# Attention units alternated with value and output projection blocks, probabilities scaled on GpSimd, and a reordered start

## The chip, the cores and the metric

One core of a Trainium2 chip runs the whole program. The metric is device time in microseconds (us) of one launch. TensorE (PE) multiplies matrices, VectorE (DVE) and ScalarE (ACT) do the elementwise work, GpSimd (POOL) small helpers, and the SP queue issues nearly all loads.

## The reference

Two layers of a backbone act on 384 tokens (128 of context, 256 latent) of width 1024. A layer is: modulated norm, SwiGLU feed-forward (1024 to 2816 and back), modulated norm, token mixer, modulated norm, a second feed-forward. Shift, scale and gate come from a conditioning vector, one for context and one for latent tokens (adaLN).

```python
h = rmsnorm(x) * (1 + sc2) + sh2
u = h @ w_in                                   # Hyena 768, neighbourhood q k v 3 x 384, grouped q 384, k v 2 x 128
y_hy = x0 * (irfft(rfft(z) * rfft(filter)) + z * skip)       # z = x1 * v after a 3-tap convolution
y_na = softmax(q @ k.T / 8 + bias, local window + cached context) @ v     # 6 heads of 64
y_gq = softmax(rope(q) @ rope(k).T / 8, window + context + sink) @ v      # 6 query heads, 2 key heads
x = x + g2 * (concat(y_hy, y_na, y_gq) @ w_out)
```

The filter comes from a small network with two sine layers and does not depend on x. Outputs are x and the new keys and values of the context tokens.

## The kernel before

Everything lies transposed: xT holds 8 chunks of 128 features by 384 tokens. Each weight block is loaded in fp32 into one of NRAW raw buffers, split into a rounded part hi and a remainder lo (`split`, L134 to L136: ACT copies, DVE subtracts), and every product is three matmuls: hi by hi, hi by lo, lo by hi (`mm3`, L294 to L298). The blocks stand in one list, `jobs` (L138 on). `get` (L178) takes the next one; `ahead` (L165) splits up to three blocks further and issues the loads up to NRAW ahead on the SP queue, which also carries the adaLN weights and the attention biases.

adaLN work is 256 "halves": a 128x1024 DVE product with sum (L199) of a loaded weight block and the activated conditioning. `ada_tick(rate)` (L242) runs them at written rates (RATE, MIXRATE, SLOTADA); `need` (L248) runs a missing one on the spot when an update or a norm wants it.

`start` (L1157) prepares the first feed-forward block: the filter network (`Filters`, L517: two sine layers, taps, spectra), the sum of squares of xT (`square_chunk`, L314, and `stats1`, L328), and the first modulations by matmul (`chunk_load`, `chunk_rows`, `chunk_cols`). Engines take their instructions in program order, so the order in `start` is the order of each queue.

`mixer` (L616) runs the six groups of the input projection. Its background work consists of generators in a list `bg`; `work(budget)` (L619) advances each by one step, front first, while the budget lasts, and `drain` runs one to its end. Generators: `hyena` (convolution, then `fft`), `na_post` (norm of q and k), `gk_post` and `gq_post` (norm and rotation of the grouped heads). After the value projection vN (L1093) q, k and Hyena are drained (L1095 to L1097). Then 15 calls of `slot` (L999) run twelve attention units as a pipeline: in slot s unit s is scored (`un_score`), unit s-1 scaled by the reciprocal of its sum (`un_norm`, L892 to L900, on DVE), the pair ending in unit s-3 multiplied with the values (`un_pv`), unit s-2 transposed (`un_turn`), unit s exponentiated (`un_exp`). A unit holds two heads and either two query blocks (context and the first latent block) or one:

```python
hs = [unit(kind, i, qi) for kind in "NG" for i in range(3) for qi in range(2)]      # L996
for c, (pr, w) in enumerate(u.pr[e]):                                              # L899
    V.tensor_scalar(pr[:, :w], pr[:, :w], rec[:, e * n + c:e * n + c + 1], None, op0=ALU.mult)
```

The grouped generators are drained after six slots. Between slots stand three blocks of the output projection (`wout_block`, L1099), after them the rest. The layer-0 filter spectrum kft[0] sits in the buffer that later holds the transposed probabilities (L587).

## Time and profile before

| what | value |
|---|---|
| median of 3 runs (lowest, highest) | 1557.25 us (1556.47, 1557.54) |
| the profiled execution, its span | 1557.04 us, 1555.3 us |
| PE busy, DVE, ACT, POOL | 1503.2, 1131.0, 671.9, 73.1 us |
| mean granted PE clock | 0.988 |
| HBM read | 257.34 MB, 167 GB/s |

The span runs from the first to the last instruction. A granted clock of 1.00 is 2.4 GHz, the other level is 1.2 GHz. Large matmuls overlap in pairs, so their rate is read from counts over a stretch. Boundaries of stretches: the first feed-forward matmul starts at 45.99 us, the layer-0 mixer at 332.85, its first unit at 433.71, the second feed-forward block at 519.58; the layer-1 mixer at 1084.69, its first unit at 1185.08, the last feed-forward block at 1270.11.

### The profile page before, as it was taken

Reading aid. Unit: us, or ns where it says so; the run is one execution under the profiler, and the core shown is the slowest. Engines: PE = TensorE matmul, PEld = TensorE weight load, DVE = VectorE, ACT = ScalarE, POOL = GpSimd, SP = SyncE. Lnnn points to the kernel's source line nnn. Section 1 sums busy time; section 2 is a strip of 40 time slices with the busy share of each in tenths; the row PEclk is TensorE's granted clock in tenths of the full one; section 3 lists DMA queues with packets and bytes.
Section 4 is the critical chain, followed back from the end, with each engine's and each line's share of the span. In section 5 each row is a group of like instructions: output and inputs, shape, how many; then the busy total and the mean of one; then the engine's idle time right before and its main releaser. Section 6 shows DMA issues by size and latency. Waiting matters only on the chain.

```text
span 1555.3 us, 22995 instructions
## 1 busy us (share of the span) xinstructions
PE 1503.2 (97%) x8616; PEld 1443.7 (93%) x8616; DVE 1131.0 (73%) x2123; ACT 671.9 (43%) x1229; POOL 73.1 (5%) x194
## 2 busy tenths in 40 slices
PE   5999999999979999999999999999998899999998
PEld 2799999999957999999999999999996699999998
DVE  5468888868877788877757898787788667544444
ACT  4533333336556454333435333334465655333221
POOL 0000000011400000000000000000141000000000
PEclk9999999999989999999999999999999999999999
DMA  8555665655422435555543566566453024443442
GB/s 288 183 209 211 223 229 205 215 196 182 116 72 75 153 140 199 210 208 205 193 159 122 190 241 233 180 231 214 157 155 100 25 97 145 139 139 109 152 153 71
DMA packets 89288, 261.46 MB, mean 168 GB/s; under 512 B 10134, under 2 KB 27096, under 8 KB 89048
## 3 DMA queue, kind: packets, MB, share of 16 engines
q1 hardware_dynamic: 88792, 258.95, 48.5%
q8 instruction: 67, 1.10, 0.3%
q0 software_dynamic: 384, 1.05, 0.2%
q14 instruction: 45, 0.37, 0.1%
HBM read 257.34 MB, written 2.62 MB: 167 GB/s over the span
## 4 chain that ended last, share of the span: by engine, by line
PE 82%; DVE 10%; ACT 5%; issue 2%; DMA 1%; SPq 0%; POOL 0%; DVEq 0%; ACTq 0%; POOLq 0%
PE up L298 14%; PE up L296 14%; PE up L297 14%; PE dn L296 8%; PE dn L297 8%; PE dn L298 8%; PE pj L296 3%; PE pj L298 2%; PE pj L297 2%; DVE wlo L136 2%; ACT whi L135 1%; DVE junk L199 1%; DVE ml L136 1%; DVE pr L900 1%; DVE pr L923 1%
## 5 line engine op out<-in xcount | busy, mean ns | idle before, releaser
L136 DVE TENSOR_TENSOR wlo<-raw,whi 128x1024 fp32r<-128x1024 f32 (+2 forms) x352 | 394.4, 1125 | 131.1 <-ACT whi L135 130.7
L296 PE MATMUL up<-mh,whi 128*128 128x384 f32 (+1 forms) x1408 | 479.3, 340 | 2.6 <-ACT mh L135 2.6
L298 PE MATMUL up<-mh,wlo 128*128 128x384 f32 (+1 forms) x1408 | 477.7, 339 | 0.7 <-DVE wlo L136 0.5
L297 PE MATMUL up<-ml,whi 128*128 128x384 f32 (+1 forms) x1408 | 477.6, 339 | 0.4 <-DVE ml L136 0.4
L135 ACT ACTIVATE whi<-raw 128x1024 fp32r<-128x1024 f32 (+2 forms) x352 | 338.7, 975 | 263.6 <-PE dn L297 125.8
L199 DVE CUSTOM_DVE_ANT_0 junk<-adaw,cb,sml 128x1024 bf16<-128x1024 f32 x256 | 332.4, 1298 | 1.9
L296 PEld LDWEIGHTS up<-mh,whi 128*128 128x128 f32 x1408 | 266.1, 189 | 4.8 <-ACT mh L135 3.3
L298 PEld LDWEIGHTS up<-mh,wlo 128*128 128x128 f32 x1408 | 266.2, 189 | 2.0 <-DVE wlo L136 2.0
L297 PEld LDWEIGHTS up<-ml,whi 128*128 128x128 f32 x1408 | 266.0, 189 | 1.6 <-DVE ml L136 1.2
L296 PE MATMUL dn<-gh,whi 128*128 128x384 f32 x704 | 237.4, 337 | 0.0
L297 PE MATMUL dn<-gl,whi 128*128 128x384 f32 x704 | 237.4, 337 | 0.0
L298 PE MATMUL dn<-gh,wlo 128*128 128x384 f32 x704 | 237.0, 337 | 0.0
L135 ACT ACTIVATE gh<-t 128x384 fp32r<-128x384 f32 x76 | 39.9, 525 | 271.8 <-DVE t L476 262.1
L297 PEld LDWEIGHTS dn<-gl,whi 128*128 128x128 f32 x704 | 132.3, 188 | 0.0
L298 PEld LDWEIGHTS dn<-gh,wlo 128*128 128x128 f32 x704 | 132.2, 188 | 0.0
L296 PEld LDWEIGHTS dn<-gh,whi 128*128 128x128 f32 x704 | 132.1, 188 | 0.0
L296 PE MATMUL pj<-whi,mh 128*128 128x384 f32 (+1 forms) x240 | 79.6, 332 | 1.1 <-DVE hyt L353 1.1
L476 DVE TENSOR_TENSOR t<-up,t 128x384 f32<-128x384 f32 x72 | 39.9, 554 | 55.2 <-PE up L298 55.0
L298 PE MATMUL pj<-whi,ml 128*128 128x384 f32 (+1 forms) x240 | 78.3, 326 | 0.0
L297 PE MATMUL pj<-wlo,mh 128*128 128x384 f32 (+1 forms) x240 | 78.1, 326 | 0.0
L136 DVE TENSOR_TENSOR gl<-t,gh 128x384 fp32r<-128x384 f32 x76 | 42.4, 558 | 45.0 <-ACT gh L135 45.0
L306 POOL TENSOR_SCALAR rs_r<-rs_r 128x3 int32<-128x3 int32 (+2 forms) x14 | 8.5, 607 | 1194.0 <-DVE rs_r L305 738.9
(220 smaller groups left out, 1585.4 us busy)
## 6 DMA issues: line engine op xcount, KB each, us to landing
raw<-w SPq DMA_DIRECT2D x184, 512.0 KB, 4.4
adaw<-ada SPq DMA_DIRECT2D x128, 512.0 KB, 3.5
raw<-w SPq DMA_DIRECT2D x64, 448.0 KB, 4.4
raw<-win SPq DMA_DIRECT2D x48, 384.0 KB, 4.0
raw<-w13a SPq DMA_DIRECT2D x32, 384.0 KB, 4.0
adw<-ada SPq DMA_DIRECT2D x32, 192.0 KB, 4.6
raw<-woa SPq DMA_DIRECT2D x16, 384.0 KB, 3.2
nab<-nab SPq DMA_DIRECT2D x24, 192.0 KB, 3.1
```

The lines of the kernel that those rows point to most:

```text
L135: S.activation(hi, src, AF.Copy)
L136: V.tensor_tensor(lo, src, hi.bitcast(F32), op=ALU.subtract)
L199: V.tensor_tensor_reduce(out=junk, in0=w, in1=cb[:, v, :], scale=scale, scalar=small("ada_b", (l * NADA + p) * KD + j), op0=ALU.mult, op1= ...
L296: T.matmul(out, ah, bh, start=start, stop=False)
L297: T.matmul(out, ah, bl, start=False, stop=False)
L298: T.matmul(out, al, bh, start=False, stop=stop)
L306: G.tensor_scalar(r.bitcast(I32), r.bitcast(I32), -1.0, float(0x5F3759DF), op0=ALU.mult, op1=ALU.add)
L476: V.tensor_tensor(t1, PQ[1][:, :NT], t1, op=ALU.mult)
L900: V.tensor_scalar(pr[:, :w], pr[:, :w], rec[:, e * n + c:e * n + c + 1], None, op0=ALU.mult)
L923: V.tensor_tensor_reduce(out=u.pr[e][0][0], in0=u.sc[e][:, :NT], in1=u.mask[e], scale=-1.0, scalar=3.0e38, op0=ALU.add, op1=ALU.min, accum ...
```

## The change

Ten of the fifteen slots get a piece of large matmuls behind them: the value projection is cut into four steps behind slots 0 to 3, and the first two groups of the output projection into pieces of 9 matmuls (one k block of one group). Hyena is not drained before the units but goes on as background, and ends before the pieces that read it. The scaling of probabilities moves from DVE to GpSimd. Rates of adaLN halves and the budgets of the background change; halves leave the slots. There are three raw buffers instead of four, and kft[0] has a tile of its own. In `start` the sine layers are cut in two so that squares stand between, the taps precede the sum of squares, the fix of tap row 0 goes from DVE to ACT, and three of eight spectrum parts are run inside the first three steps of the feed-forward block.

```diff
-NRAW = 4
+NRAW = 3
...
-RATE = ((0.76, 0.635), (0.63, 0.515), (0.69, 0.66), (0.065, 0))
-MIXRATE = ((0.75, 0, 0, 0), (0.45, 0, 0, 0))
-BUD = (1.55, 3.3, 1.3)
-SLOTADA = (6, 0.3, 0.0)
+RATE = ((0.8, 0.72), (0.63, 0.515), (0.69, 0.66), (0.065, 0))
+MIXRATE = ((0.75, 0, 0.5), (0.3, 0, 0.3))
+BUD = (2.0, 3.0, 1.9)
...
-    kft = [None, cst.tile([P, 6, HY], F32, name="kft1")]
+    kft = [cst.tile([P, 6, HY], F32, name=f"kft{l}") for l in range(DEPTH)]
...
-                for g in range(2):
-                    jobs += [(A["woa"][l, g, :, k * 768:(k + 1) * 768], 768) for k in (1, 2, 3, 0)]
+                for g, k in ((0, 1), (0, 2), (0, 3), (1, 1), (1, 2), (1, 3), (0, 0), (1, 0)):
+                    jobs.append((A["woa"][l, g, :, k * 768:(k + 1) * 768], 768))
...
-            dftl = rawp.tile([P, 1024], F32, tag="raw", name="dftl")
-            load(A["dft1"][:, 0:4], dftl.rearrange("p (i c) -> p i c", i=4))
-            self.dftl = dftl
             self.dft0 = load(A["dft0"][:, 0:2 * P], tt("dft0", w=2 * P))
+            self.dftl = [load(A["dft1"][:, i], tt("dftl", w=HY)) for i in range(4)]
...
         def first(self):
+            S.activation(junk[:, 0:1], ones[:, 0:1], AF.Sin)
             p1 = ps("f1")
             T.matmul(p1[:, :NT], self.fw1, self.feats, start=True, stop=True)
-            self.h1 = tt("h1", w=NT)
-            sin_layer(p1[:, :NT], 0, self.h1)
+            self.fb = sm("fbm", 2)
+            V.tensor_tensor(self.fb, small("fb", 0, 2), small("freq", 0, 2), op=ALU.mult)
+            self.arg = sin_arg(p1[:, :NT], 0, self.fb[:, 0:1])
 
         def second(self):
+            h1 = tt("h1", w=NT)
+            S.activation(h1, self.arg, AF.Sin)
             p2 = ps("f2")
             for l in range(DEPTH):
                 r = slice(l * HD, (l + 1) * HD)
-                T.matmul(p2[r, :NT], self.fw2[r], self.h1[r], start=True, stop=True)
-            self.h2 = tt("h2", w=NT)
+                T.matmul(p2[r, :NT], self.fw2[r], h1[r], start=True, stop=True)
             self.p2 = p2
-
-        def second_sin(self):
-            sin_layer(self.p2[:, :NT], 1, self.h2)
             self.wsd = [tt("wsd", w=HY) for _ in range(2)]
             V.tensor_tensor(self.wsd[0], self.w3[0], self.w3[1], op=ALU.add)
             V.tensor_tensor(self.wsd[1], self.w3[1], self.w3[0], op=ALU.subtract)
 
+        def third(self):
+            self.arg = sin_arg(self.p2[:, :NT], 1, self.fb[:, 1:2])
+
+        def fourth(self):
+            self.h2 = tt("h2", w=NT)
+            S.activation(self.h2, self.arg, AF.Sin)
+            self.sd = []
...
-            dec = self.decay[t].rearrange("p (o c) -> p o c", o=1)
             for l in range(DEPTH):
-                V.tensor_tensor(
-                    S2[:, :, l], pt[l].rearrange("p (i c) -> p i c", i=2), dec.to_broadcast([P, 2, HY]), op=ALU.mult
-                )
+                for i in range(2):
...
+                    for i in range(2):
+                        S.activation(S2[0:1, i, l], p0[l][0:1, :HY], AF.Copy, scale=-1.0 if i else 1.0)
...
+        def spectrum(self, ft, part):
+            which, row = ((0, False), (1, False), (0, True))[part]
...
+            for l in range(DEPTH):
+                d = kft[l][:, 3 * q + ft]
+                S.activation(d[0:1] if row else d, o[:, l * HY:(l + 1) * HY], AF.Copy, scale=sc[0:1] if row else sc)
...
+        class Project:
+            def __init__(self, n, kper):
+                self.n, self.kper, self.kb = n, kper, 0
+                self.pt = [ps(f"pj{t}", "a") for t in range(3)]
+
+            def step(self):
...
                 ahead()
-                ada_tick(MIXRATE[l][2])
+                self.kb += 1
...
+        def project(n, kper, budget):
+            pr = Project(n, kper)
+            for kb in range(KD // kper):
...
+                    work(budget)
...
+            res = pr.out()
+            work(budget)
+            return res
...
-        spare = ["a"]
+        spare = ["b"]
...
-                    V.tensor_scalar(pr[:, :w], pr[:, :w], rec[:, e * n + c:e * n + c + 1], None, op0=ALU.mult)
+                    nc.gpsimd.tensor_scalar(pr[:, :w], pr[:, :w], rec[:, e * n + c:e * n + c + 1], None, op0=ALU.mult)
...
-                pp = ps(f"pp{e}", spare[0] if TAGS[2] else "b")
+                pp = ps(f"pp{e}")
...
-            if s >= SLOTADA[0]:
-                ada_tick(SLOTADA[1 + l])
...
-        pkv = project(256, 4, lambda kb: work(BUD[1]))
+        pkv = project(256, 4, BUD[1])
         gk_it = add(gk_post(pkv), True)
-        pg = project(384, 2, whole)
-        gq_it = add(gq_post(pg))
-        vN = project(384, 2, whole)
-        nc.gpsimd.dma_start(out=A["o_nv"][l], in_=vN[0])
+        pg = project(384, 2, BUD[0])
+        gq_it = add(gq_post(pg), True)
+
+        held = {}
+
+        def piece(po, g, k):
+            kb, kk = divmod(k, 2)
+            if (g, kb) not in held:
+                held[g, kb] = get()
+            hi, lo = held[g, kb]
+            for i in range(3):
+                s = slice(kk * 384 + i * P, kk * 384 + (i + 1) * P)
+                mm3(po[i][:, :NT], (hi[:, s], lo[:, s]), Y[k], k == 2, k == 1)
+            if kk:
+                del held[g, kb]
+            ahead(state["cur"] + min(AHEAD, NSPL - len(held)))
+
         drain(q_it)
         drain(k_it)
-        drain(hy_it)
...
-        while slot_n[0] < 6:
+        pv = Project(384, 2)
+        for s in range(4):
             slot()
+            pv.step()
+        X["vN"] = pv.out()
+        nc.gpsimd.dma_start(out=A["o_nv"][l], in_=X["vN"][0])
+        po = [[ps(f"po{i}", "a") for i in range(3)]]
+        slot()
+        piece(po[0], 0, 2)
+        slot()
         drain(gk_it)
         drain(gq_it)
-        for _ in range(2):
+        for k in (3, 4, 5):
             slot()
-        spare[0] = "b"
-        po = [ps(f"po{i}", "a") for i in range(3)]
-        wout_block(po, 3, 0, 2)
-        while slot_n[0] < len(hs):
+            piece(po[0], 0, k)
             slot()
-        wout_block(po, 3, 1, 2)
-        while slot_n[0] < len(hs) + 3:
-            slot()
-        wout_block(po, 3, 2, 2)
-        wout_block(po, 3, 3, 2, False)
-        for i in range(3):
-            update(l, 5, i, po[i])
-            after(i)
+        slot()
+        piece(po[0], 0, 6)
+        slot()
+        spare[0] = "a"
+        po.append([ps(f"po{i}", "b") for i in range(3)])
+        piece(po[1], 1, 2)
+        slot()
+        for g, k in ((1, 3), (0, 7), (1, 4), (1, 5), (1, 6), (1, 7)):
+            piece(po[g], g, k)
+            work(BUD[2])
+            ada_tick(MIXRATE[l][2])
+        drain(hy_it)
+        for g in range(2):
+            for k in range(2):
+                piece(po[g], g, k)
+            for i in range(3):
+                update(l, 5, 3 * g + i, po[g][i])
+                after(3 * g + i)
+        po = [ps(f"po{i}", "ab"[i]) for i in range(2)]
+        for kb in range(2):
+            hi, lo = get()
+            for kk, i in order2(4, 2, kb == 1):
+                k = kb * 4 + kk
+                s = slice((kk * 2 + i) * P, (kk * 2 + i + 1) * P)
+                mm3(po[i][:, :NT], (hi[:, s], lo[:, s]), Y[k], k == 0, k == KD - 1)
+            if kb == 0:
+                ahead()
+                ada_tick(MIXRATE[l][2])
+        for i in range(2):
+            update(l, 5, 6 + i, po[i])
+            after(6 + i)
             if i == 0:
                 ahead()
...
     def start(j, mid=False):
+        F = filters
         if mid:
             if j in (1, 4):
                 chunk_rows((j + 2) // 3)
             return
         if j == 0:
-            F = filters
             F.load_a()
-            for c in range(KD // 2):
+            F.load_b()
+            for c in range(KD):
                 load(A["xT"][:, c], xT[c])
-            F.load_b()
-            for c in range(KD // 2, KD):
-                load(A["xT"][:, c], xT[c])
+            load(A["ct"], ct)
+            load(A["ident"], ident)
             F.load_c()
-            load(A["ident"], ident)
-            load(A["ct"], ct)
             chunk_load(0)
             issue(2)
             F.first()
-            for c in range(3):
+            for c in range(4):
                 square_chunk(c)
             F.second()
-            F.second_sin()
-            for c in range(3, KD):
+            square_chunk(4)
+            F.third()
+            for c in range(5, KD):
                 square_chunk(c)
+            F.fourth()
             S.activation(ct[:, :, 0:2], ct[:, :, 0:2], AF.Silu)
+            F.taps(0)
             r = stats1()
-            for t in range(3):
-                F.taps(t)
+            F.taps(1)
+            F.taps(2)
+            chunk_load(1)
             ada_tables(0)
-            chunk_load(1)
-            F.spectrum(0)
+            F.spectrum(0, 0)
+            F.spectrum(0, 1)
+            F.spectrum(0, 2)
             R = stats2(r)
-            start_x(0, R)
             ahead(1)
-            F.spectrum(1)
-            start_x(1, R)
             chunk_rows(0)
-            F.spectrum(2)
+            for c in range(3):
+                start_x(c, R)
+            F.spectrum(1, 0)
             chunk_cols(0)
+            F.spectrum(1, 1)
             start_h(0)
             start_h(1)
             ahead(2)
-            issue(3)
+            issue(4)
             chunk_load(2)
-            for c in range(2, KD):
+            for c in range(3, KD):
                 start_x(c, R)
             return
         if j in (2, 5):
             chunk_cols((j + 1) // 3)
         if j + 1 < KD:
             start_h(j + 1)
+        if j < 4:
+            F.spectrum(*((1, 2), (2, 0), (2, 1))[j - 1])
```

## Rows read from the trace of the kernel before

**Rows 1.** The page, part 1: busy us (share of the span), instructions.

```profile
PE 1503.2 (97%) x8616; PEld 1443.7 (93%) x8616; DVE 1131.0 (73%) x2123; ACT 671.9 (43%) x1229; POOL 73.1 (5%) x194
```

**Rows 2.** Busy us by stretch: PE, PEld, DVE, ACT, POOL; PEclk, DMA, GB/s.

```profile
73.00:332.85 259.85, 259.85 (x1485) 259.85 (x1483) 211.95 (x324) 99.18 (x150) 0.00 (x0) 1.00 0.61 218
332.85:433.71 100.86, 98.74 (x584) 95.58 (x583) 81.13 (x194) 51.67 (x105) 30.10 (x69) 1.00 0.51 156
433.71:492.07 58.36, 47.69 (x298) 32.10 (x297) 47.72 (x162) 38.43 (x115) 0.00 (x0) 0.88 0.12 42
519.58:541.18 21.60, 18.99 (x99) 18.23 (x99) 16.75 (x34) 8.55 (x18) 3.80 (x13) 0.92 0.58 199
1185.08:1242.77 57.69, 47.35 (x298) 32.17 (x298) 42.87 (x153) 38.08 (x115) 0.00 (x0) 0.88 0.13 42
1270.11:1287.69 17.58, 17.13 (x100) 16.71 (x99) 10.62 (x23) 8.41 (x18) 3.67 (x13) 1.00 0.46 156
```

**Rows 3.** PE in order of time, two units without waits: start, us, instruction.

```profile
464.58 0.92 PE L912 MATMUL sc<-kTG,qTG 64*128 64x384 f32 x4
465.43 0.87 PE L961 MATMUL pp<-ident,pr 128*128 128x128 f32 x6
466.06 0.42 PE L296 MATMUL po<-yh,whi 128*128 128x384 f32 x1
...
476.37 0.92 PE L912 MATMUL sc<-kTG,qTG 64*128 64x384 f32 x4
...
479.92 0.27 PE L963 MATMUL pp<-ident,pr 128*128 128x128 f32 x1
```

**Rows 4.** What PE waited for, whole span: us in total, times, longest.

```profile
PE gt L772 <- DVE ra L1034: 9.0, 2, 4.5
...
PE pp L961 <- DVE pr L900: 4.5, 6, 1.7
```

**Rows 5.** DVE busy with line 900 alone, layer 0's units.

```profile
433.71:492.07 58.36, 11.34 (x36) 0.88 0.12 42
```

**Rows 6.** DVE and POOL in order of time, layer 0's mixer.

```profile
340.31 1.28 DVE L199 CUSTOM_DVE_ANT_0 junk<-adaw,cb,sml 128x1024 bf16<-128x1024 f32 x1
...
340.49 1.15 POOL L306 TENSOR_SCALAR rs_r<-rs_r 128x3 int32<-128x3 int32 x1 [315.56 <-DVE rs_r L305]
...
346.55 0.20 POOL L310 TENSOR_SCALAR rs_t<-rs_t 128x3 f32<-128x3 f32 x1
...
379.71 0.23 POOL L310 TENSOR_SCALAR rs_t<-rs_t 128x18 f32<-128x18 f32 x1
```

**Rows 7.** Costliest DVE group, 519.58 to 541.18 us: busy us, mean ns.

```profile
L199 DVE CUSTOM_DVE_ANT_0 junk<-adaw,cb,sml 128x1024 bf16<-128x1024 f32 x5 | 6.5, 1290 | 0.1
```

**Rows 8.** Groups of the first feed-forward block, 73 to 332.85 us.

```profile
L199 DVE CUSTOM_DVE_ANT_0 junk<-adaw,cb,sml 128x1024 bf16<-128x1024 f32 x80 | 104.1, 1301 | 0.7
L136 DVE TENSOR_TENSOR wlo<-raw,whi 128x1024 fp32r<-128x1024 f32 (+2 forms) x65 | 76.5, 1176 | 12.7 <-ACT whi L135 12.7
L135 ACT ACTIVATE whi<-raw 128x1024 fp32r<-128x1024 f32 (+2 forms) x65 | 65.8, 1017 | 53.8 <-PE dn L297 24.5 <-issue 20.5 <-PE up L297 7.6
```

**Rows 9.** DMA issues, page part 6: KB each, median us to landing.

```profile
raw<-w SPq DMA_DIRECT2D x184, 512.0 KB, 4.4
```

**Rows 10.** The start in order of time, all engines.

```profile
9.95 10.16 SPq L103 DMA_DIRECT2D adw<-ada  x16
...
15.27 0.52 ACT L515 ACTIVATE h<-arg 128x384 f32<-128x384 f32 x1 [2.99 <-DVE arg L514]
...
19.50 1.44 PE L332 MATMUL pss<-ones,accq 128*128 128x1 f32 x6 [8.54 <-DVE accq L319]
...
28.03 2.93 PE L603 MATMUL kf<-taps,dft 128*128 128x512 f32 x6
...
39.55 3.70 PE L603 MATMUL kf<-taps,dftl 128*128 128x512 f32 x8
...
45.99 0.69 PE L296 MATMUL up<-mh,whi 128*128 128x384 f32 x1 [2.17 <-ACT mh L135]
```

114 lines of the change are left out of this document (35 added, 79 removed).

## The prediction

> **What bounds it now.** I read first the share of each engine, then the busy time by stretch, then, inside the stretches where TensorE (PE) is not full, the instructions in order of time and what they waited for. PE is busy for 97% of the span [rows 1], so the kernel is bound by PE and a change that neither adds nor drops large matmuls can only win or lose the time in which PE waits or runs at the low clock. Where the weights stream, nothing is left: the first feed-forward block issues 1485 matmul records in 259.85 us, 0.175 us each, at full clock, with PE busy throughout [rows 2]. The holes are elsewhere. The attention stretches of the two layers last 58.36 and 57.69 us with PE busy for 47.7 and 47.4 at a granted clock of 0.88, a mix of the 2.4 and 1.2 GHz levels [rows 2].
>
> How much of such a stretch is excess: a key/query pair (a unit with two query blocks and one with a single one) costs PE 1.48 us for scores and transposes of the small unit and 480.19 - 476.37 = 3.82 us for scores, values and transposes of the large one when nothing is waited for, 5.3 us [rows 3]. Six pairs are 31.8 us; the 54 output-projection matmuls placed in the stretch are 54 x 0.175 = 9.45; nine transposes of the rotated queries some 0.9. That is 42.2 of 58.36 us: 16.2 us of excess in layer 0, 15.5 in layer 1. A visible piece of it is the wait for the rotated queries, 4.5 us in each layer, and smaller ones for the scaled probabilities [rows 4].
>
> **The change, part by part.**
>
> *Alternation.* The value projection (4 blocks of 18 matmuls, 3.15 us each) now stands between the first four units, and six half-blocks of the output projection (9 matmuls, 1.6 us) between the later ones; query rotation runs ahead of the key work and of Hyena; Hyena's transforms, formerly run dry before the first unit, slide into the units. PE work is the same. After it a pair with one half-block costs PE 6.9 us, one with two value blocks 11.6; ScalarE was busy 38.43/6 = 6.4 us per pair and VectorE 47.72/6 = 8.0 us [rows 2], of which the scaling of probabilities is 11.34/6 = 1.9 [rows 5]; without it VectorE has 6.1. So no engine is longer than PE in a pair, and the waits that remain are these: the last rotation is still drained in one go after the sixth unit (I keep 2.5 of 4.5 us); five half-blocks read the attention output made one step earlier, and I allow each 0.5 us, the wait for probabilities now being 4.5 us in 6 [rows 4]; about 1 us where a short unit follows a long one. Sum 6 us per layer, so 10.2 and 9.5 are gained: 20 us. Bounds: 3 per layer (the bubbles move) and 16 (all filled).
>
> *Hyena before the units.* The stretch ahead holds 2.1 us of PE idle in layer 0 [rows 2], mostly around the transforms; with other work beside them I take 1 us per layer, 2 together (0 to 4).
>
> *Scaling on GpSimd.* Per layer 24 instructions of 128x384 and 12 of 128x128 leave VectorE and go to GpSimd, which the trace shows only with tiny operands: 0.20 us for 3 columns and 0.23 for 18 undisturbed [rows 6], so 2 ns per column and an estimate of 0.96 us for 384 and 0.45 for 128: 4.7 us per pair, under the 6.9 of PE. Lower end is VectorE's own 1.9 per pair. Upper end: the same 3-column instruction took 1.15 us when it was issued during a 1.28 us VectorE operation on two SBUF tensors, and ended with it [rows 6]; if all six instructions of a pair wait 0.95 us so, 10.4 us per pair. I take 4.7, since most VectorE work of these units reads PSUM; the scaling is then hidden, because a unit's transposes come two steps after its scores.
>
> The Trainium skill, "SBUF — State Buffer", section "Who interferes with whom", says that GpSimd and a VectorE instruction with two SBUF inputs take one port pair in turn, whole instruction by whole instruction. The stretched rows above agree. By that rule the relief of VectorE can be given back entirely, which is the second case below.
>
> *Faster adaLN halves in layer 0.* The rates 0.76/0.635 become 0.8/0.72: 36 x 1.6 + 20 x 1.44 = 86 halves in the first feed-forward block where 80 ran [rows 8], 6 more of 1.3 us; VectorE goes from 211.95 to 220 us of 259.85 [rows 2], so PE still covers it; were the cover gone it would cost 8 us. In return the halves that the update had to run on the spot disappear: five of them, 6.5 us of VectorE, stand in the 21.60 us after layer 0's mixer [rows 7], where layer 1 needs 17.58 for the same matmuls [rows 2]. I take the whole difference, 4 us (2 to 5). Dropping the ticks in the units frees VectorE there; the new ticks in the projection tail have its matmuls beside them: nothing.
>
> *Start.* Today the second sine runs at 15.27, yet PE waits 8.54 us, until 19.50, for the sum of squares, which stands ahead of the taps in its queue [rows 10]. The second argument now needs no new bias product and the first no table load, which I price at 1 us together: second sine at 14.3, done at 14.8; the taps follow it at once, ahead of the sum. From there PE has work without a hole: taps and sum 8.5 us (19.50 to 28.03), the first spectrum 2.9, the spread of the root 0.75, the row matmuls 3.1, two parts of the second spectrum 3.5, the columns 0.7 (all as they ran before), then some 2.2 us until the first operand is there. Together 21.6: first feed-forward matmul at 36.4 instead of 45.99. But 3 spectrum parts (12 records; eight of the like took 3.70 us, 0.46 each, so 5.5 us) move behind it and take PE time there. Net 9.6 - 5.5, 4 us. Bounds 1 (the first modulation weights, 16 loads, are all issued only at 20.1 and the start sticks to them [rows 10]) and 9. Row fixes move from VectorE to ScalarE, which idles there; the sine table is loaded while the inputs travel; four loads instead of one for the transform add about 1.5 us to the SP queue ahead of those weights, inside that bound.
>
> *Three raw buffers instead of four.* A weight block is issued when its buffer is free. Its cycle is landing 4.4 [rows 9], ScalarE copy 1.0, VectorE difference 1.2, plus waiting behind one or two 1.3 us halves [rows 8] and in the SP queue: 8 to 10 us, against 3 x 4.2 = 12.6 us in which PE uses three blocks (24 matmuls each). The split also runs three blocks ahead. Nothing, then; what it costs without that cover is the last case. The own tile for the spectrum of layer 0 and the new order of output weights cost nothing: they only lift a wait, and each load is as long as before.
>
> Sum: 20 + 2 + 4 + 4 = 30 us against the profiled execution's own 1557.04 us (span 1555.3 and 1.7 around it), which lies 0.2 us under the median of the runs: 1527 us. At the lower bounds 3+3+0+2+1 = 9 us are gained, 1548; at the upper ones 16.2+15.5+4+5+9 = 50, 1507.
>
> **Rivals.**
>
> *Forecast*, 1527 us (own range 1510 to 1541): 0.58.
>
> *The relief is eaten by the shared port.* GpSimd's 28.4 us per layer (24 x 0.96 + 12 x 0.45) and VectorE's two-input work (weight differences, rotations) exclude each other; if 11 of them collide, VectorE is as loaded as today, 8 us per pair, longer than PE's 6.9, and 6 x 1.1 = 7 us per layer of the gain go, with the short units waiting for late transposes for the rest. Then only the start and the adaLN part pay: 1557 - 8 = 1549, or a little less: 0.17. For it: the 1.15 us of [rows 6]; against: the scores' operation on VectorE reads PSUM and a mask, one SBUF tensor.
>
> *More is filled*: the bubbles all but vanish and the start reaches its upper bound: 1557 - 32 - 4 - 5 - 9 = 1507, or 1505 to 1510: 0.14. For it: PE's clock of 0.88 in the units goes back to 1.00 once nothing starves it; against: two units in a row still lack a block between them.
>
> *Slower: three raw buffers starve PE.* It decides when a buffer's cycle passes 12.6 us. In the stretches with many halves VectorE works in long runs, and two halves more before a difference would bring 12 us, an SP queue held by a modulation load one or two more. At 13.6 us each block comes 0.33 us late: over some 210 blocks in the three feed-forward blocks that carry halves 70 us, less the 30 gained: 1597. 0.07. Against it: today no such block has PE waiting, and the split runs ahead.
>
> *Nothing moves*: gains of the units cancelled by waits of the new order, within 0.2%, which is about what a measurement of this kernel can tell from no change (3 us): 0.04.
>
> **The numbers.** The likeliest case gives 1527. From 1505 to 1550 lie the forecast, nearly all of the two neighbours, and left out are the slow case, the unchanged one and a little at either edge, about 0.15. Faster by over 0.2%: 0.58 + 0.17 + 0.14 = 0.89; same 0.04; slower 0.07.
>
> **What would show it.** Right: first feed-forward matmul near 36 us; PE at full clock through the units, with no wait of more than 3 us ahead of the rotated queries; GpSimd instructions of about 1 us that end before the transposes; no VectorE halves in the 20 us after layer 0's mixer. Wrong: PE waits named after GpSimd in the units (port), ScalarE's weight copy waiting for DMA in the feed-forward blocks (buffers), or a first feed-forward matmul that waits for the modulation rows (start).

## The result, and the profile after

The changed kernel takes 1579.24 us (median of 4 runs, 1577.55 to 1582.27), the kernel before 1556.93 beside it (1556.47 to 1557.54): a ratio of 1.0145, with a 95% interval of 1.0128 to 1.0163. The forecast was 1527 with a range of 1505 to 1550; the kernel is slower by 22 us, not faster by 30. The profiled execution took 1582.27 us, 3 above the median, with a span of 1580.5.

Page of the changed kernel, part 1, to set beside [rows 1]:

```profile
span 1580.5 us, 23068 instructions
PE 1518.8 (96%) x8616; PEld 1446.2 (92%) x8616; DVE 1109.9 (70%) x2048; ACT 675.9 (43%) x1237; POOL 148.8 (9%) x266
```

VectorE was relieved as intended and GpSimd took the work, yet the span grew by 25.2 us. To see where, I cut each layer at marks in PE's timeline: **units** from the second group of query and key transposes (qkt) to the last product with the values (py), which takes in the value projection both where it stands ahead of the units and where it stands between them; **tail** from there to the next feed-forward block's first matmul (up); **stretch after the mixer** from there to the matmul that spreads the next norm's root (pr). Busy time by stretch, columns as in [rows 2]; first the kernel before, units, tail and stretch after the mixer of layer 0, then of layer 1:

```profile
405.11:492.14 87.03, 74.88 (x451) 57.18 (x449) 68.84 (x219) 50.35 (x140) 8.95 (x23) 0.92 0.24 75
492.14:519.58 27.44, 27.44 (x157) 27.44 (x157) 17.68 (x36) 16.30 (x37) 0.00 (x0) 1.00 0.41 129
519.58:540.83 21.25, 18.64 (x98) 18.02 (x97) 16.75 (x34) 8.55 (x18) 3.80 (x13) 0.92 0.58 199
1156.45:1242.83 86.38, 74.56 (x451) 57.27 (x449) 63.97 (x210) 50.01 (x140) 8.84 (x23) 0.92 0.24 75
1242.83:1270.11 27.28, 27.28 (x157) 27.28 (x157) 16.51 (x34) 16.14 (x36) 0.00 (x0) 1.00 0.28 92
1270.11:1287.26 17.15, 16.70 (x97) 16.41 (x97) 10.62 (x23) 8.41 (x18) 3.67 (x13) 1.00 0.46 155
```

The same of the changed kernel:

```profile
404.26:499.49 95.23, 81.55 (x469) 61.12 (x467) 53.03 (x171) 51.06 (x141) 46.62 (x59) 0.93 0.23 72
499.49:523.62 24.13, 24.13 (x139) 24.13 (x139) 17.44 (x32) 10.55 (x21) 0.00 (x0) 1.00 0.39 137
523.62:552.41 28.79, 21.92 (x97) 19.18 (x97) 17.44 (x39) 13.69 (x31) 3.17 (x13) 0.82 0.26 87
1167.66:1262.67 95.01, 81.71 (x469) 61.37 (x467) 52.98 (x171) 51.05 (x141) 46.44 (x59) 0.91 0.23 73
1262.67:1286.81 24.14, 24.14 (x140) 24.14 (x140) 16.65 (x31) 11.52 (x24) 0.00 (x0) 1.00 0.36 121
1286.81:1312.40 25.59, 19.91 (x97) 17.26 (x97) 15.82 (x36) 12.72 (x29) 3.77 (x13) 0.93 0.37 118
```

PE issues 18 matmuls more in the changed units (469 against 451): half-blocks of the output projection that stood in the tail, 18 x 0.175 = 3.15 us. Units and tail together grew from 114.47 to 119.36 us in layer 0 and from 113.66 to 119.15 in layer 1, **5 us each**. The stretch after the mixer grew by **7.5 and 8.4 us** for the same 97 matmuls, with the granted clock at 0.82 in layer 0: PE sat idle, then ran partly at 1.2 GHz. The rest: the first feed-forward matmul 6.0 us earlier (39.99 against 45.99), that block 2.5 longer (289.38 against 286.86), Hyena's part of layer 0 2.6 longer. 4.9 + 5.5 + 7.5 + 8.4 - 6.0 + 2.5 + 2.6 = 25.4, the difference of the spans to 0.2.

What PE waited for in the changed kernel (us in total, times, longest), to set beside [rows 4]:

```profile
PE pp L960 <- POOL pr L899: 13.0, 16, 2.1
PE gt L774 <- DVE ra L1032: 9.3, 2, 4.6
PE up L293 <- DVE xT L373: 6.4, 5, 1.9
PE up L293 <- ACT mh L132: 3.7, 3, 2.4
PE up L293 <- ACT whi L132: 3.4, 3, 1.8
```

The largest wait is new: transposes (pp) wait for probabilities (pr) that GpSimd scales. The wait for the rotated queries (gt), of which the forecast kept 2.5 of 4.5 us, is whole. The third and fifth are new too, and stand in the stretch after the mixer: feed-forward matmuls wait for a residual update (xT) and a weight split (whi).

GpSimd's scaling by shape (busy us, mean ns), where [rows 5] had 36 x 0.315 us on VectorE for a layer:

```profile
L899 POOL TENSOR_SCALAR pr<-pr,nm 128x384 f32<-128x384 f32 x48 | 61.4, 1284 | 65.5 <-DVE nm L896 29.5 <-PE sc L914 12.0 <-ACT pr L945 7.5
L899 POOL TENSOR_SCALAR pr<-pr,nm 128x128 f32<-128x128 f32 x24 | 18.4, 767 | 0.0
```

The SP queue of the changed kernel after the last unit of layer 0, in order of time (start, us, issue):

```profile
495.96 0.33 SPq L100 DMA_DIRECT2D raw<-wob  x1
505.54 0.33 SPq L100 DMA_DIRECT2D adaw<-ada  x1
505.97 0.37 SPq L100 DMA_DIRECT2D raw<-wob  x1
508.94 0.33 SPq L100 DMA_DIRECT2D adaw<-ada  x1
509.36 0.38 SPq L100 DMA_DIRECT2D raw<-w13a  x1
512.61 0.33 SPq L100 DMA_DIRECT2D adaw<-ada  x1
513.03 32.90 SPq L100 DMA_DIRECT2D raw<-w13a  x7
```

What the queue itself waited for there (499 to 556 us), first the splits (wlo) that free a weight's buffer, then the halves (mod):

```profile
SPq L100 <- DVE wlo L133: 35.0, 7, 10.2
SPq L100 <- DVE mod L196: 14.6, 3, 9.2
```

And the residual updates on VectorE there (two segments of a chunk in each row):

```profile
513.64 0.73 DVE L373 SCALAR_TENSOR_TENSOR xT<-po,mod,xT 128x128 f32<-128x128 f32 x2
516.76 0.74 DVE L373 SCALAR_TENSOR_TENSOR xT<-po,mod,xT 128x128 f32<-128x128 f32 x2
...
524.17 0.74 DVE L373 SCALAR_TENSOR_TENSOR xT<-po,mod,xT 128x128 f32<-128x128 f32 x2
...
530.47 0.73 DVE L373 SCALAR_TENSOR_TENSOR xT<-po,mod,xT 128x128 f32<-128x128 f32 x2
```

Two things are new against the kernel before. Six halves run on VectorE between the last unit and the first update (between 502.9 and 512.6 us, 1.28 us each), and their loads (adaw) stand ahead of weight blocks in the queue, where each waits until VectorE has run the half that frees its buffer; which of the two costs time is settled below. And six updates run one behind the other at 3.1 us or more each (a chain between VectorE and ScalarE: update, square, norm factor, split), since both projection groups now end together; the splits of the next weights stand between and behind them.

### The profile page after: what moved, and what is told of

It is laid out like the page before. It is cut to its first block, busy times and chain, and to the rows that moved or that the text cites. A ratio compares the mean times of both kernels' runs of the same rounds, so it can differ in the third digit from the quotient of the medians.

```text
span 1580.5 us, 23068 instructions
## 1 busy us (share of the span) xinstructions
PE 1518.8 (96%) x8616; PEld 1446.2 (92%) x8616; DVE 1109.9 (70%) x2048; ACT 675.9 (43%) x1237; POOL 148.8 (9%) x266
## 4 chain that ended last, share of the span: by engine, by line
PE 82%; DVE 7%; ACT 6%; POOL 2%; issue 2%; DMA 1%; SPq 0%; DVEq 0%; ACTq 0%; POOLq 0%
PE up L293 14%; PE up L294 14%; PE up L295 14%; PE dn L294 8%; PE dn L293 8%; PE dn L295 8%; PE pj L293 2%; PE pj L295 2%; PE pj L294 2%; DVE wlo L133 2%; POOL pr L899 1%; ACT whi L132 1%; PE sc L911 1%; PE kf L593 1%; PE hy L293 1%
## 5 line engine op out<-in xcount | busy, mean ns | idle before, releaser
L899 POOL TENSOR_SCALAR pr<-pr,nm 128x384 f32<-128x384 f32 x72 | 78.8, 1112 | 65.5 <-DVE nm L896 29.5
L473 DVE TENSOR_TENSOR t<-up,t 128x384 f32<-128x384 f32 x72 | 39.9, 554 | 49.8 <-PE up L295 49.7
```

The costliest lines, as they stand in the source:

```text
L473: V.tensor_tensor(t1, PQ[1][:, :NT], t1, op=ALU.mult)
L899: nc.gpsimd.tensor_scalar(pr[:, :w], pr[:, :w], rec[:, e * n + c:e * n + c + 1], None, op0=ALU.mult)
```

## The experiments

All times are medians; ratios are to the kernel before on the same chip, with the 95% interval. Units, tail and stretch after the mixer (marks as above, layer 0 / layer 1, us) come from the profile of each kernel. The kernel before (with halves or without) has 156 matmuls in its tail, all others 138; the 18 stand in the units there.

| kernel | units | tail | stretch after the mixer | time |
|---|---|---|---|---|
| before | 87.0 / 86.4 | 27.4 / 27.3 | 21.3 / 17.2 | 1556.9 |
| after | 95.2 / 95.0 | 24.1 / 24.1 | 28.8 / 25.6 | 1579.2 |
| after, scaling on VectorE | 88.1 / 87.4 | 24.1 / 24.3 | 27.9 / 25.5 | 1562.6 |
| after, pipeline deeper | 85.4 / 84.9 | 24.1 / 24.2 | 28.3 / 25.7 | 1564.3 |
| both of these | 90.5 / 91.0 | 24.2 / 24.2 | 27.7 / 25.4 | 1569.6 |
| after, four raw buffers | 95.1 / 96.5 | 24.3 / 24.2 | 27.8 / 25.5 | 1583.2 |
| after, group 0 first | 95.4 / 95.5 | 26.7 / 26.7 | 24.4 / 22.0 | 1577.5 |
| after, no halves in the tail | 95.4 / 94.9 | 24.1 / 24.2 | 27.1 / 24.5 | 1578.6 |
| after, group 0 first, no halves | 95.2 / 95.2 | 24.3 / 24.3 | 23.1 / 20.0 | 1568.2 |
| before, halves in the tail | 87.9 / 86.4 | 27.4 / 27.3 | 25.3 / 21.7 | 1565.8 |
| VectorE, group 0 first, four raw | 91.3 / 89.2 | 26.7 / 28.2 | 24.1 / 19.8 | 1564.6 |
| that, new order of the units | 81.7 / 81.7 | 28.3 / 28.3 | 23.0 / 19.8 | 1547.1 |
| that, no halves in the tail | 81.5 / 81.9 | 24.3 / 24.4 | 19.5 / 17.8 | **1533.1** |
| that, three raw buffers | 79.3 / 79.7 | 24.3 / 24.3 | 22.9 / 19.8 | 1536.4 |

### The units: late results from GpSimd

Scaling back on VectorE, all else as changed:

```diff
-                    nc.gpsimd.tensor_scalar(pr[:, :w], pr[:, :w], rec[...], None, op0=ALU.mult)
+                    V.tensor_scalar(pr[:, :w], pr[:, :w], rec[...], None, op0=ALU.mult)
```

> The changed kernel with the scaling of probabilities back on VectorE, nothing else. Theory A (the scaling on GpSimd, 6.07 us per pair of units instead of 1.9, lengthens the chain from scores to transposes, and TensorE waits in every unit): the stretch of the units falls from 94 to about 84 us in each layer, the run from 1579 to about 1559. Rival (the new order itself holds TensorE, half-blocks waiting for the attention output just made): the stretch stays above 91 us and the run above 1573.

1562.63 us, 1.0030 [1.0018, 1.0042]. 16.6 us come back, most of them in the units (7.1 and 7.7), and the wait for GpSimd is gone. Only 2.1 and 1.7 us of those 7.1 and 7.7 are idle PE. The rest is PE being busy for longer with the same 469 instructions (81.55 and 81.71 us against 76.49 and 75.78), at a granted clock of 0.93 and 0.91 against 0.96 and 0.98: late results cost clock on top of the wait. But the units only reach the kernel before: with the 3.15 us of moved matmuls in mind they are 2 us better, not 10.

The reverse, the same line of the kernel before moved to GpSimd:

> The kernel before with the scaling on GpSimd and nothing else. Theory A: without large matmuls beside the units the longer chain is fully exposed, some 4 us per pair less what overlaps: 20 to 45 us slower than before, 1577 to 1602. Rival (GpSimd's work lies beside other work): within 5 us of 1557.

1563.69, 1.0038 [1.0023, 1.0052]: units 4.4 us longer in layer 0 and 0.2 in layer 1. Both theories missed. The edit is the same in both layers, so the price of GpSimd is no constant of the instruction; the slots differ in the halves they carry (four on VectorE in layer 0, none in layer 1), and whether that makes the difference isn't shown. PE waits for GpSimd here too (4.5 and 4.7 us), but the relief of VectorE shortens the wait for the rotated queries from 4.5 us to 1.7 and 1.4, and PE's idle time in the units falls by 1 us in each layer. The 4.4 us of layer 0 are PE busy for 5.5 us longer, at a granted clock of 0.89 instead of 0.92.

Whether the wait goes when the result has more time was tried next: scaling left on GpSimd, transposes three slots behind the scores and values four, a sixteenth slot, and the half-blocks one slot later:

```diff
-            if 0 <= s - 3 < len(hs) and hs[s - 3].qi:
-                un_pv(hs[s - 3])
-            if 0 <= s - 2 < len(hs):
-                un_turn(hs[s - 2])
+            if 0 <= s - 4 < len(hs) and hs[s - 4].qi:
+                un_pv(hs[s - 4])
+            if 0 <= s - 3 < len(hs):
+                un_turn(hs[s - 3])
```

> The changed kernel with the scaling on GpSimd as it is, but with the transposes three slots behind the scores and the values four, in place of two and three. Theory chain: GpSimd has time enough (46 of 94 us busy) and only its result comes late, so one slot more hides it: of the 15 to 16 us that scaling on VectorE gave back, at least 10 come back here, 1565 to 1569 us. Rival throughput: GpSimd's pairs of 6.07 us follow each other, or it holds VectorE up at the port; then a longer pipeline brings under 5 us, 1575 to 1580.

1564.28, 1.0047 [1.0029, 1.0064]. As the theory of the chain had it: 15 us come back with GpSimd as busy as before (46.3 us in each set of units). Waits of this kernel's PE:

```profile
PE gt L774 <- DVE ra L1032: 8.0, 2, 4.0
PE up L293 <- DVE xT L373: 6.4, 5, 1.9
PE up L293 <- ACT mh L132: 5.7, 3, 2.3
```

The transposes' wait for GpSimd has left the top of the list; that for the rotated queries has not. The units won 9.8 and 10.1 us, but the feed-forward blocks behind them lost 2.5 and 1.2: a feed-forward matmul at 561.03 us waited 1.7 us for its operand instead of 0.6, and the granted clock was 0.50 from 561.7 to 565.1 us.

Is it the deeper pipeline or GpSimd that wins? The same kernel with VectorE scaling:

> The run with GpSimd and the pipeline one slot deeper, but with the scaling on VectorE. It tells what the scaling on GpSimd is worth once its result is not waited for. Theory relief: VectorE is 12 us busier in each set of units, and the waits for VectorE come back; 88 and 87 us for the units as in the run on VectorE without the deeper pipeline, against 85.4 and 84.9 with GpSimd, so about 1568 us. Rival slack: VectorE has slack in the units (53 of 94 us busy in the changed kernel), so the deeper pipeline alone gives what that run gained: units at 85 to 85.5 us, time 1562 to 1566.

1569.62, 1.0083 [1.0068, 1.0098]: units 90.5 and 91.0. The theory of relief holds: with the deeper pipeline GpSimd is worth 5 to 6 us for each set of units. In the time 5.3 us in all are left of it: by the profiles Hyena's part is 1.6 us longer with GpSimd and the feed-forward work after the mixers 2.5 and 1.4. VectorE's slack on average (62.6 of 90.5 us busy) did not help: PE waits for particular VectorE results, 8.4 us for the values' remainder (yl) and 8.7 for the rotated queries over the span, as with two steps (7.7 and 8.7), and new are 3.6 for an operand of the transforms (yc).

### The start, and three raw buffers

The kernel before with the new `start` and `Filters`, the own tile for kft[0] and three raw buffers; rates, mixer and weight order as before:

```diff
-NRAW = 4
+NRAW = 3
...
-    kft = [None, cst.tile([P, 6, HY], F32, name="kft1")]
+    kft = [cst.tile([P, 6, HY], F32, name=f"kft{l}") for l in range(DEPTH)]
...
```

> The kernel before with the new start (filter, squares and spectra reordered), the own tile for layer 0's spectrum and three raw buffers; rates, mixer and units as before. Theory: the start gives 6 us ahead of the first feed-forward matmul and pays 2.5 to 3 back in the block, and three buffers cost nothing: 1553 to 1554. Rival C (three raw buffers starve the feed-forward blocks): 1557 or above, with ScalarE waiting for weights and TensorE behind it.

1558.02, 1.0006 [0.9997, 1.0015]: no difference. The start comes 8.05 us earlier (37.94), the block behind it gives 2.5 back, and the two stretches after the mixers lose 3.05 and 2.2. So three buffers cost some 5 us, as the rival's time had it, but not in the long feed-forward stretches, which kept their length (279.0 against 279.3 us for the block ahead of layer 1's mixer).

The fourth buffer given back to the changed kernel, with three 384-column work tiles fewer to make room:

```diff
-NRAW = 3
-NTP = 50
+NRAW = 4
+NTP = 47
```

> The changed kernel with the fourth raw buffer back (and 47 projection buffers in place of 50, to make room). Theory raw buffers: with three buffers the first up-projection transfers of the next feed-forward network stay behind the splits that the mixer's last updates hold back; the kernel before with three of them lost 3.05 and 2.2 us in the two stretches after the mixers, so here these fall from 28.8 and 25.6 us to about 26 and 23, and the time to about 1574 us. Rival: the order of the updates alone holds the splits back, a fourth buffer only waits with them; the stretches stay within 1 us and the time at 1579.

1583.22, 1.0169 [1.0154, 1.0184]. A miss: the stretches fell by 1.0 and 0.1 us only. In this kernel something else ends last there. The profile is longer by 1.5 us in layer 1's units and by 2.5 in the feed-forward work after each mixer; whether the three missing work tiles do that isn't shown.

### The tail and the stretch after the mixer: three covers, one behind the other

Group 0 of the output projection finished first and its three updates run beside group 1, as in the kernel before:

```diff
-                for g, k in ((0, 1), (0, 2), (0, 3), (1, 1), (1, 2), (1, 3), (0, 0), (1, 0)):
+                for g, k in ((0, 1), (0, 2), (0, 0), (0, 3), (1, 1), (1, 2), (1, 3), (1, 0)):
...
+        for k in (6, 7):
+            piece(po[0], 0, k)
...
+        for i in range(3):
+            update(l, 5, i, po[0][i])
+            after(i)
+        for k in (2, 3, 4, 5, 6, 7, 0, 1):
+            piece(po[1], 1, k)
```

> The changed kernel with the tail of the mixer in another order: group 0 of the output projection is finished and its three chunks updated before group 1's eight half-blocks run, then group 1's three chunks, then the last group. Theory B (six chunk updates in one row, each a chain of VectorE and ScalarE of 3.1 us, with the next weight splits queued behind them, arrive after TensorE has run out): the stretch from the first feed-forward matmul after the mixer to the spread of the root falls from 29.2 and 26.0 us to about 19 in each layer, the run to about 1563. Rival (weights arrive late because only three raw buffers are there): no gain over 3 us.

1577.46, 1.0127 [1.0112, 1.0142]. A miss in size: the stretches shrank by 4.4 and 3.6 us, but the tails grew by 2.5 each. Together with VectorE scaling and the fourth buffer:

> The changed kernel with the scaling on VectorE, group 0 of the output projection finished and updated first, and four raw buffers. Theory: the three costs add up: 16 us in the units, 2 to 4 us in the tail and after the mixers, 5 us of the raw buffers, so about 1555 to 1558 us, no slower than the kernel before, with 21 and 18 us after the mixers and 88 us for each set of units. Rival: the units on VectorE delay the updates behind them, so that the parts overlap and the time stays at 1561 us or above.

1564.59, 1.0048 [1.0029, 1.0067]. The parts did not add up, as the rival said. Then the halves of the tail alone, on the changed kernel:

```diff
-MIXRATE = ((0.75, 0, 0.5), (0.3, 0, 0.3))
+MIXRATE = ((0.75, 0, 0), (0.3, 0, 0))
```

> The changed kernel without the modulation halves in the projection tail (third mixer rates 0), nothing else. Theory SP queue: a load of modulation weights waits in the SP queue for its buffer until VectorE has run a half, and the weight blocks behind it wait too (9 us without an issue after the first load of the last output block); without them the two stretches after the mixers fall from 28.8 and 25.6 us to 22 to 24 and 19 to 21, the time from 1579 to 1566 to 1570 us. Rival update chain: the six updates one behind the other (3.1 us each) hold the splits back with or without halves; under 3 us in all, 1576 or above.

1578.55, 1.0134 [1.0118, 1.0149]: under 1 us, as the rival said, so by this run the halves were innocent. But the same halves added to the kernel before:

```diff
-MIXRATE = ((0.75, 0, 0, 0), (0.45, 0, 0, 0))
+MIXRATE = ((0.75, 0, 0, 0.5), (0.45, 0, 0, 0.3))
```

> The kernel before with modulation halves in its projection tail, at the rates of the changed kernel (0.5 and 0.3 for each block of groups 1 and 2), nothing else. Theory SP queue: its loads of modulation weights hold the weight blocks up in the tail; tail and stretch after the mixer grow by 3 to 6 us in each layer (48.7 and 44.4 us before), 1563 to 1569 us; in layer 0 up to 4 us come back, since five halves no longer run after the mixer. Rival: with the updates spread over the tail the queue is fed early enough, and the time stays within 3 us of 1557.

1565.76, 1.0058 [1.0043, 1.0073], slower by 8 to 9 us, with 4.1 and 4.5 in the two stretches after the mixers: the range of the SP queue theory. Its mechanism is another matter. The SP queue of this kernel, and that of the kernel before at the same place, once from 491 us on and once from 498 us on:

```profile
497.22 0.33 SPq L103 DMA_DIRECT2D raw<-w13a  x1
509.01 0.33 SPq L103 DMA_DIRECT2D adaw<-ada  x1
509.43 1.28 SPq L103 DMA_DIRECT2D raw<-w13a  x2
```

```profile
497.22 24.59 SPq L103 DMA_DIRECT2D raw<-w13a  x6
```

```profile
507.74 14.07 SPq L103 DMA_DIRECT2D raw<-w13a  x5
```

The row of six is merged and hides a pause: in the kernel before, too, nothing goes out between 497.22 and 507.74, until a weight split has freed a buffer. The load of modulation weights delays the next weight block by 1.7 us, from 507.74 to 509.43. And no copy of weights feels it. ScalarE's waits in tail and stretch after the mixer of layer 0, with the halves:

```profile
ACT sq L317 <- DVE xT L376: 17.8, 7, 7.3
ACT whi L135 <- PE po L297: 1.9, 1, 1.9
ACT accq L317 <- DVE xT L376: 1.7, 1, 1.7
ACT yh L135 <- PE py L987: 1.6, 1, 1.6
```

None is for a load; the block issued at 509.43 landed at 513.39 and was copied at 524.68. What ScalarE waits for is the residual update (xT) on VectorE. VectorE's first and last half ahead of group 1's first update, that update, and below it the same update in the kernel before:

```profile
507.63 1.34 DVE L199 CUSTOM_DVE_ANT_0 junk<-adaw,cb,sml 128x1024 bf16<-128x1024 f32 x1
514.68 1.28 DVE L199 CUSTOM_DVE_ANT_0 junk<-adaw,cb,sml 128x1024 bf16<-128x1024 f32 x1
515.89 0.74 DVE L376 SCALAR_TENSOR_TENSOR xT<-po,mod,xT 128x128 f32<-128x128 f32 x2
```

```profile
510.85 0.74 DVE L376 SCALAR_TENSOR_TENSOR xT<-po,mod,xT 128x128 f32<-128x128 f32 x2
```

Four halves stand ahead of this update in VectorE's order, and it comes 5.0 us later; the splits of the next weights stand behind the updates and move with them. So the trace speaks for the halves' own time on VectorE and against the queue. No run has the loads without the halves. Both edits at once on the changed kernel:

> The changed kernel with group 0 of the output projection finished and updated first and without the halves in the projection tail; three raw buffers, scaling on GpSimd as it is. Theory two covers: the chain of late updates and the loads held in the SP queue end at about the same time, so that each alone hides the other; with both gone tail and stretch after the mixer fall from 52.9 and 49.7 us to about 46 and 44, the time from 1579 to 1565 to 1568 us. Rival raw buffers: with three buffers nothing is regained beyond the 2 us of the order: 1574 or above.

1568.15, 1.0068 [1.0053, 1.0083]. Tail and stretch together fall from 52.9 to 47.4 and from 49.7 to 44.2: 11.0 us, where each edit alone had given under 3. That is the theory of two covers in its sizes: each edit alone hides the other. The second cover is the halves; that it is their loads, as the expectation said, isn't shown. The third is the raw buffer: in the kernel with the new order of updates and no halves (below) going from four to three buffers costs 3.4 and 2.1 us in the stretches after the mixers, on the changed kernel it had been worth 1.0 and 0.1. Update order, halves and missing buffer end close to each other, and each alone hides behind the others.

Late results and halves mended together, order and buffers as changed (pipeline deeper, third rates 0):

> The changed kernel with the pipeline of the units one slot deeper and without the halves in the projection tail; the scaling stays on GpSimd, the raw buffers are three, the order of the updates is the new one. Theory of two causes: 15 us (late results) and 10 to 12 us (halves) add up: 1552 to 1555 us, some 3 us faster than the kernel before. Rival: more is lost elsewhere (raw buffers, update order): above 1558.

1560.32, 1.0021 [1.0012, 1.0031]: not below 1558, as the rival said; the update chain still holds the stretches at 26.7 and 24.5 us.

### A version faster than both

From the kernel with VectorE scaling, group 0 first and four raw buffers, first the rotation alone, one step more of it ahead of the grouped units:

```diff
             pv.step()
+        next(gq_it)
         X["vN"] = pv.out()
```

> The kernel with VectorE, group 0 first and four raw buffers (1564.6 us) with one step more of the query rotation ahead of the grouped units, and the half-blocks where they were. It divides the 17.5 us between that run and the best one. Theory: the wait for the rotated queries (4.3 us) goes and nothing else, 4 to 5 us for each layer: units at 87 and 85 us, time 1555 to 1557. Rival: the waits for the values take its place and the half-blocks' place is what counts: under 2 us for each layer, 1561 or above.

1560.34, 1.0019 [1.0005, 1.0034]: 1.6 and 2.5 us in the units, between the two theories. Then each half-block one slot later as well, so that it does not follow the step that makes its operand:

```diff
-        slot()
-        piece(po[0], 0, 2)
         slot()
+        slot()
         drain(gk_it)
         drain(gq_it)
+        piece(po[0], 0, 2)
         for k in (3, 4, 5):
             slot()
-            piece(po[0], 0, k)
             slot()
+            piece(po[0], 0, k)
```

> The kernel of the run with VectorE, group 0 first and four raw buffers, with the half-blocks of the output projection one slot later and one more step of the query rotation ahead of the grouped units. Theory: TensorE's waits for the values (3.8 us) and the rotated queries (4.3 us) in each set of units are put there by the order of the steps alone; both go, 5 to 8 us for each layer, 1541 to 1548 us, faster than the kernel before. Rival: VectorE sets the pace of the units (its work only moves), the waits come back under another name and the gain is under 3 us in all.

1547.08, 0.9934 [0.9919, 0.9948], faster than the kernel before. The units fall to 81.7 us in both layers, 9.6 and 7.5 us under the kernel it came from. Then the halves out of the tail:

> The best kernel so far (1547 us) without the modulation halves in the projection tail and in the projections (third mixer rates 0 in place of 0.5 and 0.3). Theory ticks: the halves stand between the last residual updates and the weight splits on VectorE (one of 1.28 us ahead of the update of chunk 6, the split of the last block late by 1.6 us); without them the tail falls from 28.25 to about 27 us and the stretch after it from 22.97 and 19.84 to about 21.5 and 18.5, the time to 1541 to 1543 us. Rival: the halves that are left out fall due at the update itself and cost the same there: within 2 us of 1547.

**1533.06, 0.9844 [0.9829, 0.9859]**: 14 us where 5 were expected. The cause is the one that the expectation named, halves between the updates and the splits on VectorE, but it counted one of them and not all. Tail and stretch after the mixer of layer 0, by stretch, without halves:

```profile
480.76:505.08 24.32, 24.32 (x138) 24.16 (x139) 15.64 (x33) 14.97 (x34) 0.00 (x0) 1.00 0.26 83
505.08:524.60 19.52, 17.87 (x97) 16.31 (x97) 15.46 (x31) 9.06 (x19) 3.68 (x13) 1.00 0.51 178
```

Group 1's first update with the halves (last unit ends at 482.62 us) and without (480.76):

```profile
506.15 0.74 DVE L373 SCALAR_TENSOR_TENSOR xT<-po,mod,xT 128x128 f32<-128x128 f32 x2
```

```profile
496.86 0.74 DVE L373 SCALAR_TENSOR_TENSOR xT<-po,mod,xT 128x128 f32<-128x128 f32 x2
```

That is 23.5 and 16.1 us after the last unit: 7.4 us, with six halves ahead of it or none. In layer 1, with four, it is 4.8 us, and with the fifth the mixer's last update comes 6.0 us later. Tail and stretch together are 7.4 and 6.0 us shorter without them. With the halves, too, no copy of weights waited for a load there. The clock stays at 1.00. The same with three raw buffers:

> The best kernel (1533 us) with three raw buffers and 50 projection buffers as in the changed kernel. Theory: three buffers cost as in the kernel before, 2 to 3 us after each mixer, 1537 to 1539 us. Rival: without the halves the SP queue is early enough and three buffers suffice: within 2 us of 1533.

1536.39, 0.9865 [0.9849, 0.9882]: 5.5 us more after the mixers, of which the units, 2 us shorter in each layer, return most; this kernel has three work tiles more, and whether they do it isn't shown. Finally GpSimd in these kernels, with the deeper pipeline, with halves and without:

> The best kernel so far (1547 us) with the scaling on GpSimd and the pipeline one slot deeper. Theory relief: with its latency hidden the scaling on GpSimd takes 2 to 3 us off each set of units, 79 us against 81.7, and the time is 1541 to 1544 us. Rival: VectorE is not the limit there any more; the sixteenth slot lengthens the end by 1 to 2 us and the time is 1547 to 1551.

> The best kernel so far (1533 us) with the scaling on GpSimd and the pipeline one slot deeper. Theory relief: units at 79 to 80 us against 81.5 and 81.9, nothing else moves: 1528 to 1531 us. Rival: what the units gain is lost in the blocks after them again, as it was in the run with halves (1549.6 against 1547.1): 1533 to 1537.

1549.58, 0.9958 [0.9943, 0.9972], and 1536.91, 0.9877 [0.9861, 0.9894]. The units are 1.4 to 2.7 us shorter than with VectorE (80.1 and 79.0; 80.1 and 79.4), yet the medians are 2.5 and 3.9 us longer, with a spread of up to 7.7 us. The profiled spans differ by little (1530.7 against 1531.9), so what the medians add is not in these profiles; that stays open.

## Why the prediction was wrong, point by point

**"The scaling is then hidden, because a unit's transposes come two steps after its scores": this step failed**, and cost 15 to 17 us. The duration was off by a third and two thirds (1.28 us for 0.96, 0.77 for 0.45), a pair of units 6.65 us on average for 4.7 (6.07 undisturbed): inside the bounds and under PE's 6.9 for a pair. Throughput was not the question. What counts is when a head's scalings end: PE had come to its transposes up to 2.1 us earlier. In that longest case the reciprocals were ready at 420.25 us, GpSimd still had the roots of a norm to finish until 421.72, and the first scaling ended at 422.96. One slot more, with nothing made faster, took the wait away. The sign that the prediction gave to the port, PE waits named after GpSimd, did appear, but for another reason: one slot more took it away with GpSimd as busy as before. Two steps are a distance in code; the step should have been priced in us, from reciprocal to first transpose.

**The shared port** was a rival at 7 us a layer. VectorE's busy time in the units of layer 0 fell by 9.4 us (62.44 with scaling there, 53.03 without), not by the 11.3 of [rows 5]: 2 us were given back. It is seen on a line with two SBUF tensors, the scaling of the grouped queries, in the changed kernel and in the one with VectorE scaling (ns: least, median, most):

```profile
L1043 DVE TENSOR_TENSOR pj<-pj,gqg x6: 615/824/825, 425.8 to 1213.4; 128x384 f32<-128x384 f32 x6
```

```profile
L1043 DVE TENSOR_TENSOR pj<-pj,gqg x6: 557/558/560, 423.2 to 1197.7; 128x384 f32<-128x384 f32 x6
```

By the rule of the Trainium skill, "SBUF — State Buffer", section "Who interferes with whom", such an instruction and a GpSimd instruction that reads SBUF hold each other up; the 824 ns for 558 agree. The total given back is 2 us a layer, where the rival had 7.

**Alternation, 20 us**: as written in the change it gave 4.3 (with VectorE scaling, units and tail: 114.5 to 112.2 and 113.7 to 111.6), below my lower bound of 3 a layer. Two allowances failed: the rotation wait stayed at 4.3 us a layer (I kept 2.5), and the half-blocks waited 7.7 us over both layers for operands made one step before them (I allowed 5). In all, PE stands idle for 11.6 us in each layer's units, where the forecast left 6 and the kernel before had 12.2 and 11.8: the bubbles moved. That a later kernel with rotation and half-blocks moved and no halves in the tail (three raw buffers) takes 103.6 and 104.0 us for units and tail, 20.5 less than before, is the size of the forecast, but it took further edits and does not bear the forecast out. There was also a plain miscount: the stretch of [rows 2] held 36 output-projection matmuls, not 54, so the excess to be won was 3.15 us larger than I wrote.

**"The new ticks in the projection tail have its matmuls beside them: nothing": this step failed.** I asked whether PE has work beside a half, and not what stands behind it on VectorE: the residual updates, and behind them the splits of the next weights. Six halves in layer 0 moved group 1's first update by 7.4 us in the best kernel, and the end of the stretch with it. In time they cost 8 to 9 us in the kernel before and 14 in the best one. Two of my expectations put this down to their loads in the SP queue; in tail and stretch the traces show no weight copy that waits for a load, neither in the kernel before with halves nor in the one of 1547 us. In the changed kernel, with three buffers, one copy of an output block waited 3.8 us.

**The reordered tail was costed at nothing, too.** Only the order of the weights was looked at, not that six updates now end together. With the halves and the missing buffer it makes the 7.5 and 8.4 us after the mixers.

**Three raw buffers: "nothing"** was right where I looked and wrong after the mixers: 2.1 to 3.4 us each. The slow rival had them starve PE in the feed-forward blocks, 70 us; there the sign I named did appear, ScalarE's weight copies waiting for DMA (2.1 us in all in the kernel before):

```profile
ACT whi L132 <- DMA raw<-w: 120.8, 55, 5.9
```

but PE never waited for these copies there: 264.19 us for the long stretch of layer 0's second block against 264.60. The rival had the direction right (slower), but its mechanism was not the cause.

**Faster halves, 4 us**: 86 of them ran in the first block, as forecast. But the slots had carried five that the change dropped, so of the five on the spot after layer 0's mixer four remained (third rates 0); with the tail's ticks they ran there instead. Nothing was gained.

**Start, 4 us net**: right in the net, 3.5 us in the profiled execution, with both terms smaller than forecast: the first feed-forward matmul at 39.99 for 36.4, the moved spectra 2.5 us for 5.5. In fifteen of the other sixteen profiles with the new start it comes at 35.7 to 38.3 (40.4 once), and the block behind it is 2.5 to 4.1 us longer than before. PE's wait for xT does not make the difference (4.8 us here, 5.1 in the run with VectorE scaling, which starts at 36.1); the six matmuls of the first spectrum took 4.42 us here and 2.93 there. Why isn't shown.

**Hyena beside other work, 2 us**: not seen. Of the 2.1 us of idle PE that I counted, 0.6 stand ahead of the units' mark (405.11 us) and 1.5 behind it, where they can't be told from the alternation. The part ahead of the mark was 2.6 us longer in layer 0 and unchanged in layer 1; with four raw buffers it is 72.3 to 72.4 us in every kernel, before included, and with three 72.8 to 74.9.

The profile held the failed steps in plain sight: GpSimd behind a chain to the transposes, updates paced by a two-engine chain, and halves that share VectorE's order with those updates.

## What to carry to other kernels

When work moves to a slower engine, price the latency from its first input to the consumer in PE's order, not its share of the time; if throughput fits, one more pipeline stage is the repair. Background work costs what it delays on its own engine: beside a busy PE the halves looked free, and ahead of the updates on VectorE each cost nearly its own 1.3 us. A merged row (six issues in 24.59 us) can hide a pause, so compare the same stretch from a later start before a queue is called held up. Where several limits end within a microsecond or two of each other, taking one away shows next to nothing: remove them in pairs, or add one to the kernel that has none, before calling any innocent.

## What was not expected of the hardware

GpSimd's scaling (ns: least, median, most; two shapes) in the changed kernel, and one unit pair of it in order of time:

```profile
L899 POOL TENSOR_SCALAR pr<-pr,nm x72: 600/1245/1666, 421.7 to 1257.6; 128x384 f32<-128x384 f32 x48, 128x128 f32<-128x128 f32 x24
```

```profile
471.04 6.07 POOL L899 TENSOR_SCALAR pr<-pr,nm 128x384 f32<-128x384 f32 x6 [6.32 <-PE sc L914]
```

The least, 600 ns, is a 128x128, the median a 128x384: (1245 - 600) / 256 = 2.5 ns for a column more, against VectorE's 0.54 (medians of 0.418 and 0.280 us for the two shapes in the run with VectorE scaling). The 2 ns a column that the small operations of [rows 6] gave were a fifth too low. PE had waited 1.9 us until 528.23, with 1.8 and 1.2 us more in the next 6; from 530.2 to 540.4 us the granted clock was 0.50, the 1.2 GHz level, and 0.82 over the stretch after the mixer. So an idle microsecond cost more than itself: of the 7.5 us that layer 0's stretch grew, 4.3 are idle PE (6.87 us for 2.61), the rest is the same 97 matmuls being busy for 21.92 us in place of 18.64.
